# Unscaled operands for a seven-product gated MLP: the sums move into attention's last projection, and GpSimd stops computing there

## The chip, the core and the metric

The kernel runs on one core of a Trainium2 chip. It computes a small decoder trunk on 512 tokens. The metric is the device time of one execution in microseconds (us), given as the median of several runs.

A core has several engines that run side by side, each with its own list of instructions: TensorE (PE in the profile) multiplies matrices and has a separate step that loads weights (PEld); VectorE (DVE) and ScalarE (ACT) compute element by element; GpSimd (POOL) can compute too and issues some of the transfers; SyncE (SP) issues the others. Engines wait for each other by semaphores. On-chip memory has 128 partitions, so a tile "128x512" holds 128 rows of 512 numbers. Products are summed up in PSUM, a memory of its own from which DVE and ACT read.

## The reference

Two layers. The first has a mixer (a linear recurrence and a pooling branch), the second a convolution module in its place, and each layer goes on with cross-attention and a gated MLP. The change lies in the MLP and in the last projection of attention. Cut to these:

```python
def rms_norm(x, g):
    y = x * lax.rsqrt(jnp.mean(x * x, axis=-1, keepdims=True) + EPS)
    return y * g

def cross_attn(x, mem, norm, mem_norm, wq, wk, wv, wo):
    ...
    o = jnp.einsum('bhqk,bkhd->bqhd', p, v).reshape(Bn, S, D_MODEL)
    return o @ wo

def conv_ffn(x, norm, w_up, dw_w, dw_b, w_down):
    h = rms_norm(x, norm) @ w_up
    g = causal_dwconv(h[..., :D_FF], dw_w, dw_b)      # width 3
    u = h[..., D_FF:]
    return (jax.nn.gelu(g) * u) @ w_down

for layer in range(2):
    x = x + (mixer_ab if layer == 0 else conformer_conv)(x, ...)
    x = x + cross_attn(x, ...)
    x = x + conv_ffn(x, ...)
return rms_norm(x, final_norm)
```

The width of the model is 1024, that of the MLP 3072, the tokens are 512. All is float32.

## The kernel before

**Layout and exactness.** Activations lie transposed: the residual stream is eight tiles `X[0]` to `X[7]`, each of 128 channels by 512 tokens. A float32 operand is split into a *high part* (a copy rounded to the type that PE takes, made by ACT at L162) and a *low part* (what the rounding left, a subtraction on DVE, or on POOL where the code asks for it, L163). `mm3` (L168 to L170) makes one product of three matmuls: high by high, high by low, low by high. A 512-token matmul has 512 columns, one of a half has 256.

**The norm.** Attention's last projection (`back`) adds each finished chunk to `X[n]` and feeds it to the next norm, `Norm.feed`: L189 makes the high part of gain times X, L190 its low part (both kept in `act` tiles as `norm.x`), and L198 sums the squares on DVE. `norm.x` does not hold the scale, the reciprocal root of the mean square, which is the same for all channels of a token. The scale `norm.r` is made later (`rstd`: a split of the sum, two matmuls with a matrix of 1/1024 at L229 and L230, a root on ACT at L255, a reciprocal on DVE), and what was computed from `norm.x` is multiplied by it afterwards.

**The MLP** (`ffn`) has 24 chunks of 128 gate channels and as many value channels. Chunks 0 to 3 are made in the *opening*: eight plain products `start(0)` to `start(7)`, gate and value of each chunk in turn, of 24 matmuls of 512 columns. Their weights are the pieces of `wup`: a load, a high part, a low part (L577, L580), the first two before the opening. Between the products stand the width-3 convolution (`tap_steps`), the GELU, the product with `norm.r` (on POOL) and that with the value.

Chunks 4 to 23 are made by one *unit* each, which computes gate and value together as a product of two-by-two blocks with seven block products instead of eight (Winograd's form of Strassen's scheme; the value's sign is turned, so that the weights need sums only). The weight blocks are a11, a12 (gate) and a21, a22 (value), of 512 channels; from them come s3 = a11 + a21, s1 = a21 + a22, s2 = s3 + a22, s4 = s2 + a12. These sums are made by DMAs that add into memory, issued on POOL (L543 to L549), each as soon as the block before it has been split; the raw tile that holds a11 is overwritten by s3, s2 and s4 in turn, the one that holds a21 by s1. The operands on the other side are blocks of 512 channels by 256 tokens: B11, B21, B22, and the sums T1 = B11 - B12, T3 = B22 - B12, T2 = -T3 - B11 and T4 = -T2 - B21 (rows are halves of the channels, columns halves of the tokens). Class `Seven` makes all seven in the opening, from X times gain *times the scale* (`operand`, L478 to L508): eight scaled chunks (L493), two differences on POOL, two on DVE, and the high and low parts of all seven, those of T1 to T4 with their low parts on POOL. They lie in 14 of the 15 `big` tiles.

A unit's block products come in the order B11, B21, T2, T3, T1, B22, T4 (`m(...)`), 12 matmuls of 256 columns each; DVE combines their results by halves (L610). Between T3 and T1, and behind T4, stand two *down products* of 12 matmuls of 512 columns, which multiply finished chunks with a piece of `wdown` and add to X. So a unit has 84 matmuls of 256 columns and 24 of 512. Each slot between two products also splits blocks for the next units (`ahead`: high part on ACT, low part on DVE, sum DMA on POOL).

**What sets the order.** Inside `ffn` the order on PE, ACT, DVE and POOL is the order of the program text (`manual_schedule`); SP's loads, and everything outside, are ordered by a planner with priorities. Each of these engines works strictly in its order, so that one instruction that waits holds up all behind it on that engine. Tiles come from pools that are reused in turn: 32 `act` tiles, 15 `big` tiles, four `whi` and four `wlo`, three `raw`, eight `tmp`, five PSUM tiles `mm` and two `aux`.

**GpSimd** computes in the opening (low parts of weight blocks, products with the scale, differences, low parts of T1 to T4) and in the second layer's convolution module. In the units it only issues the sum DMAs.

Of the kernel before, what the change touches and what calls it, by code (L numbers as in the profile page):

```python
# [58 lines left out]
def trunk(ctx: ExitStack, tc: tile.TileContext, I: dict, out: list):  # L59
# [111 lines left out]

    def blk(w, i, n=P):
        hi, lo = w
# [51 lines left out]
    def mean_all(s, n=T):  # L225

        hi, lo = split(s, act_r()[:, :n], act_r()[:, :n])
# [146 lines left out]
    def attention(layer, norm, mem, nxt):  # L374
# [82 lines left out]
        back(0, range(4, 6))  # L457
        back(1, range(6))
        transpose(3)
        back(2, range(6))  # L460
        mix(3)
        for n in range(3):
            back(n, range(6, C))
        for n in range(3, C):
            back(n, range(C))


    class Seven:
# [6 lines left out]
        def __init__(self, norm):  # L475
            self.norm = norm
            self.x = [(big_r(), big_r()) for _ in range(7)]

        def operand(self, h):

            two = lambda t: t.rearrange("p (a b) -> p a b", a=2)
            f = [big_f(), wp.tile([P, D], F32, tag="wlo", name=nm("scaled"))]
            at = slice(h * T, (h + 1) * T)
            t1, t2, t3, t4 = [two(tmp_f()) for _ in range(4)]
            (b11, b12), (b21, b22) = [(two(t)[:, :, :M], two(t)[:, :, M:]) for t in f]

            def part(j, t, eng=None):
                split(t, two(self.x[j][0][:, at]), two(self.x[j][1][:, at]), eng)

            for k in range(2):  # L490
                for i in range(2):
                    c = 4 * k + 2 * h + i
                    V.scalar_tensor_tensor(  # L493
                        f[k][:, i * T : (i + 1) * T], X[c], col(self.norm.gain[0], self.norm.gain[1] + c), self.norm.r,
                        op0=ALU.mult, op1=ALU.mult,
                    )
            G.tensor_tensor(t3, b22, b12, op=ALU.subtract)
            G.tensor_tensor(t1, b11, b12, op=ALU.subtract)
            yield
            part(self.B11, b11)  # L500
            part(self.B21, b21)
            part(self.B22, b22)
            yield
            V.scalar_tensor_tensor(t2, t3, -1.0, b11, op0=ALU.mult, op1=ALU.subtract)
            V.scalar_tensor_tensor(t4, t2, -1.0, b21, op0=ALU.mult, op1=ALU.subtract)
            part(self.T2, t2, G)
            part(self.T3, t3, G)
            yield  # L508
            part(self.T1, t1, G)
            part(self.T4, t4, G)  # L510

        def product(self, ps, w, j):
            for c in range(4):
                at = slice(c * M, (c + 1) * M)
                mm3(ps, blk(w, c * P), (self.x[j][0][:, at], self.x[j][1][:, at]), c == 0, c == 3)
            return ps

    class Blocks:
# [15 lines left out]
        def part(self, name, eng=None):  # L534
# [4 lines left out]
            of = {"a12": self.a12, "a22": self.a22, "s1": self.z}.get(name, self.r)  # L539
            self.w[name] = split(of, self.hi[:, at], self.lo[:, at], eng) if at else split(of, eng=eng)  # L540
# [10 lines left out]
    def ffn(layer, norm, nxt):  # L551
        ys = {}

        def taps_of(c, g):
            y = tmp_f()
            for _ in tap_steps(c, g, y):
                pass
            return y

        def tap_steps(c, g, y):  # L560
            dw = lambda j: col("f_dw_w", (layer * 3 + j) * CF + c)
            A.activation(y, g, AF.Identity, scale=dw(2), bias=col("f_dw_b", layer * CF + c))
            yield
            for s in (1, 2):
                V.scalar_tensor_tensor(y[:, s:], g[:, : T - s], dw(2 - s), y[:, s:], op0=ALU.mult, op1=ALU.add)  # L565
            yield
# [775 lines left out]
```

## Time and profile before

| | |
|---|---|
| time, median of 3 runs | 1500.24 us (1499.22 to 1501.97) |
| the profiled execution | 1499.24 us |
| its span in the trace | 1497.5 us |
| mean granted clock of PE | 0.99 |
| PE busy | 1457.3 us (97%), 8388 matmuls |
| DVE busy | 1102.4 us (74%) |
| ACT busy | 729.3 us (49%) |
| POOL busy | 344.5 us (23%), 336 instructions |

Where the stages lie in the span of the trace: attention's last projection of the first layer ends at 365 us, the opening of the first MLP follows up to 418 us (the first matmul of the first unit starts at 418.02), then come its 20 units up to 738 us. The second layer's convolution module and attention follow, and its MLP begins at 1093.5 us.

How to read the rows. A row of a single instruction gives its start and its duration in us, the engine, the line of the kernel, the operation, the program's names (written from <- read) and the shapes; what it waited for stands in brackets at the end, with the waiting time. A row of a group gives the number of instructions and three numbers in ns: the shortest, the middle and the longest. A row "a <- b: x, n, y" of the waits says that instructions of kind a waited for b for x us in sum, n times, y at the longest. Busy times of an engine are shares of the span; only the time in which nothing else could go on is worth anything when it is removed.

### The profile page before, as it was taken

Reading aid. Unit: us, or ns where it says so; the run is one execution under the profiler, and the core shown is the slowest. Engines: PE = TensorE matmul, PEld = TensorE weight load, DVE = VectorE, ACT = ScalarE, POOL = GpSimd, SP = SyncE. Lnnn points to the kernel's source line nnn. Section 1 sums busy time; section 2 is a strip of 40 time slices with the busy share of each in tenths; the row PEclk is TensorE's granted clock in tenths of the full one; section 3 lists DMA queues with packets and bytes.
Section 4 is the critical chain, followed back from the end, with each engine's and each line's share of the span. In section 5 each row is a group of like instructions: output and inputs, shape, how many; then the busy total and the mean of one; then the engine's idle time right before and its main releaser. Section 6 shows DMA issues by size and latency. Waiting matters only on the chain.

```text
span 1497.5 us, 21974 instructions
## 1 busy us (share of the span) xinstructions
PE 1457.3 (97%) x8388; PEld 1260.8 (84%) x8388; DVE 1102.4 (74%) x1684; ACT 729.3 (49%) x1162; POOL 344.5 (23%) x336
## 2 busy tenths in 40 slices
PE   8999999999989999999999998999998999999997
PEld 7988788887779999999887666888876999999997
DVE  7876765657878777777776995766678877877765
ACT  7568743434445444544445336544444444454433
POOL 0012310001542222222006852300036222222111
PEclk9999999999999999999999999999999999999999
DMA  8523233203257777776426653321233777877741
GB/s 298 162 87 97 85 126 99 71 28 112 72 145 180 168 170 164 187 164 154 136 97 176 162 162 109 112 97 57 71 84 98 184 169 159 179 181 164 171 119 57
DMA packets 75641, 198.99 MB, mean 133 GB/s; under 512 B 8464, under 2 KB 9488, under 8 KB 75536
## 3 DMA queue, kind: packets, MB, share of 16 engines
q1 hardware_dynamic: 52208, 155.36, 33.3%
q0 software_dynamic: 23040, 41.95, 16.7%
q8 instruction: 66, 1.08, 0.3%
q14 instruction: 39, 0.32, 0.1%
q10 hardware_dynamic: 288, 0.27, 0.1%
HBM read 145.13 MB, written 2.10 MB: 98 GB/s over the span
## 4 chain that ended last, share of the span: by engine, by line
PE 74%; DVE 7%; issue 5%; DMA 3%; ACT 3%; POOL 2%; SPq 0%; ACTq 0%; POOLq 0%; DVEq 0%
PE mm L168 18%; PE mm L170 18%; PE mm L169 18%; PE aux L168 6%; PE aux L169 6%; PE aux L170 6%; PE aux L1110 1%; DVE tmp L565 1%; DVE wlo L163 1%; DVE wlo L580 1%; DVE act L163 1%; DMA raw<-wa 1%; POOL tmp L701 1%; DMA big<-in_wdown 1%; ACT whi L162 1%
## 5 line engine op out<-in xcount | busy, mean ns | idle before, releaser
L170 PE MATMUL mm<-act,wlo 128*128 128x512 f32 (+1 forms) x829 | 323.4, 390 | 8.8 <-DVE wlo L580 6.2
L168 PE MATMUL mm<-act,whi 128*128 128x512 f32 (+1 forms) x829 | 323.6, 392 | 0.5 <-ACT act L162 0.5
L169 PE MATMUL mm<-act,whi 128*128 128x512 f32 (+1 forms) x829 | 323.1, 390 | 0.0
L168 PE MATMUL mm<-bigr,act 128*128 128x256 f32 x832 | 237.1, 285 | 2.2 <-DVE tmp L610 1.9
L162 ACT ACTIVATE whi<-raw 128x1024 fp32r<-128x1024 f32 (+1 forms) x161 | 152.0, 948 | 178.7 <-PE mm L169 94.9
L169 PE MATMUL mm<-bigr,act 128*128 128x256 f32 x832 | 237.1, 285 | 0.0
L170 PE MATMUL mm<-bigr,act 128*128 128x256 f32 x832 | 236.7, 284 | 0.0
L170 PEld LDWEIGHTS mm<-act,wlo 128*128 128x128 f32 x829 | 156.8, 189 | 42.6 <-DVE wlo L580 7.9
L168 PEld LDWEIGHTS mm<-act,whi 128*128 128x128 f32 x829 | 156.7, 189 | 37.8 <-issue 3.3
L163 DVE TENSOR_TENSOR wlo<-raw,whi 128x1024 fp32r<-128x1024 f32 (+1 forms) x139 | 152.5, 1102 | 43.6 <-ACT whi L162 41.5
L169 PEld LDWEIGHTS mm<-act,whi 128*128 128x128 f32 x829 | 156.8, 189 | 32.1 <-DVE act L163 1.3
L162 ACT ACTIVATE act<-raw 128x512 fp32r<-128x512 f32 x176 | 108.5, 623 | 154.0 <-DMA raw<-raw 103.0
L168 PEld LDWEIGHTS mm<-bigr,act 128*128 128x128 f32 x832 | 160.9, 193 | 4.6 <-issue 2.2
L169 PEld LDWEIGHTS mm<-bigr,act 128*128 128x128 f32 x832 | 161.0, 193 | 1.9 <-issue 0.2
L168 PE MATMUL aux<-act,whi 128*128 128x512 f32 x407 | 159.8, 393 | 2.6 <-ACT act L162 1.3
L170 PE MATMUL aux<-act,wlo 128*128 128x512 f32 x407 | 158.8, 390 | 3.3 <-DVE wlo L163 3.3
L169 PE MATMUL aux<-act,whi 128*128 128x512 f32 x407 | 159.6, 392 | 2.3 <-DVE act L163 2.3
L170 PEld LDWEIGHTS mm<-bigr,act 128*128 128x128 f32 x832 | 160.9, 193 | 0.2 <-issue 0.2
L163 POOL TENSOR_TENSOR wlo<-raw,whi 128x1024 fp32r<-128x1024 f32 (+1 forms) x22 | 51.8, 2366 | 415.2 <-ACT whi L162 415.1
L163 DVE TENSOR_TENSOR act<-raw,act 128x512 fp32r<-128x512 f32 x162 | 111.2, 688 | 37.8 <-ACT act L162 37.2
L610 DVE TENSOR_TENSOR tmp<-mm,tmp 128x256 f32<-128x256 f32 x280 | 113.5, 419 | 2.1 <-PE mm L170 2.1
L169 PE MATMUL mm<-bigr,whi 128*128 128x256 f32 x392 | 111.0, 283 | 0.0
(269 smaller groups left out, 2714.3 us busy)
## 6 DMA issues: line engine op xcount, KB each, us to landing
raw<-wa POOLq DMA_DIRECT2D x120, 256.0 KB, 5.0
big<-in_wdown SPq DMA_DIRECT2D x42, 512.0 KB, 5.4
wa<-in_wpair SPq DMA_DIRECT2D x80, 256.0 KB, 4.2
raw<-in_wpair SPq DMA_DIRECT2D x40, 512.0 KB, 5.1
raw<-in_pw SPq DMA_DIRECT2D x24, 512.0 KB, 3.7
raw<-in_win SPq DMA_DIRECT2D x20, 512.0 KB, 3.3
raw<-raw POOLq DMA_DIRECT2D x40, 256.0 KB, 4.4
raw<-in_wv SPq DMA_DIRECT2D x16, 512.0 KB, 5.2
```

The source lines that it names most:

```text
L162: A.activation(hi, src, AF.Copy)
L163: (eng or V).tensor_tensor(lo, src, hi.bitcast(F32), op=ALU.subtract)
L168: PE.matmul(ps, wh, xh, start=first, stop=False)
L169: PE.matmul(ps, wh, xl, start=False, stop=False)
L170: PE.matmul(ps, wl, xh, start=False, stop=last)
L565: V.scalar_tensor_tensor(y[:, s:], g[:, : T - s], dw(2 - s), y[:, s:], op0=ALU.mult, op1=ALU.add)
L580: V.tensor_tensor(w[2], w[0], w[1].bitcast(F32), op=ALU.subtract)
L610: V.tensor_tensor(out, a, b, op=ALU.add)
L701: G.tensor_tensor(y[c], y[c], norm.r, op=ALU.mult)
L1110: return PE.matmul(accs[c][32 * j : 32 * j + 32, s:], taps[c][:, 4 * g + j], hs[c][1][j][:, : T - s], start=s == 0, stop=g == PE_GROUPS[c] ...
```

## The change

It has five parts.

1. *Operands without the scale.* B11, B21 and B22 are no longer made: `product` takes halves of `norm.x`, which exists anyway (chunks 0 to 3 and 4 to 7 are the two halves of the channels, columns 0 to 255 and 256 to 511 those of the tokens). T1 to T4 are made from gain times X without the scale. The scale is then applied in each unit to the combined gate and value, two products of 512 columns on DVE (L616 and L620 of the changed kernel).
2. *The sums in attention's last projection.* `sums(k)` makes one quarter (128 of 512 channels) of all four T operands from chunks k and k + 4. The projection ends its chunks in the order 0, 4, 1, 5, 2, 6, 3, 7, and behind each of the first three pairs stands one call; the fourth call is in the opening, behind `start(4)`. The split of the sum of squares is made ahead of `start(0)`.
3. *No arithmetic on GpSimd in the MLP.* Low parts, products with the scale and differences go to DVE; POOL issues DMAs only.
4. *High parts ahead of low parts.* `part` is split into `high` (ACT) and `low` (DVE and the sum DMA), and in most slots the text has the high parts first, or a slot earlier than the low parts. The weight pieces get a class `Piece` with the same two halves. The s blocks now lie in `big` tiles, both parts in one, where they were two `act` tiles.
5. *Pieces of work carried over.* The gating of a chunk is a generator, `left`, of which the next unit runs the rest; the sum of a down product with X is carried as `due`. The next raw load of a unit moves from behind product B11 to behind T3.

The core of the diff:

```diff
@@ back, behind the scores and mixes
+        seven = Seven(nxt)
+        for k in range(4):
+            for n in (k, k + 4):
+                back(n, range(6 if n in acc else 0, C))
+            if k < 3:
+                for _ in seven.sums(k):
+                    pass
+        return seven
@@ class Seven
-            self.x = [(big_r(), big_r()) for _ in range(7)]
+            self.t = [(big_r(), big_r()) for _ in range(4)]
-        def operand(self, h):
...
+        def sums(self, k):
+            f = [tmp_f(), tmp_f()]
+            for i in range(2):
+                c = k + 4 * i
+                A.activation(f[i], X[c], AF.Copy, scale=col(self.norm.gain[0], self.norm.gain[1] + c))
+            (b11, b12), (b21, b22) = [(x[:, :M], x[:, M:]) for x in f]
+            t13, t24 = tmp_f(), tmp_f()
+            t1, t3, t2, t4 = t13[:, :M], t13[:, M:], t24[:, :M], t24[:, M:]
+            V.tensor_tensor(t3, b22, b12, op=ALU.subtract)
+            V.tensor_tensor(t1, b11, b12, op=ALU.subtract)
             V.scalar_tensor_tensor(t2, t3, -1.0, b11, op0=ALU.mult, op1=ALU.subtract)
             V.scalar_tensor_tensor(t4, t2, -1.0, b21, op0=ALU.mult, op1=ALU.subtract)
+            at = slice(k * M, (k + 1) * M)
+            for (hi, _), t in zip(self.t, (t1, t2, t3, t4)):
+                A.activation(hi[:, at], t, AF.Copy)
             yield
+            for (hi, lo), t in zip(self.t, (t1, t2, t3, t4)):
+                V.tensor_tensor(lo[:, at], t, hi[:, at].bitcast(F32), op=ALU.subtract)
 
         def product(self, ps, w, j):
             for c in range(4):
-                at = slice(c * M, (c + 1) * M)
-                mm3(ps, blk(w, c * P), (self.x[j][0][:, at], self.x[j][1][:, at]), c == 0, c == 3)
+                if j >= self.T1:
+                    x = blk(self.t[j - self.T1], c * M, M)
+                else:
+                    x = blk(self.norm.x[c if j == self.B11 else c + 4], M if j == self.B22 else 0, M)
+                mm3(ps, blk(w, c * P), x, c == 0, c == 3)
@@ class Blocks: part(name, eng) becomes high(name) and low(name)
+                both = big_r()
+                self.w[name] = both[:, :T], both[:, T:]
+            A.activation(self.w[name][0], self.block(name), AF.Copy)
...
+        def low(self, name):
+            hi, lo = self.w[name]
+            V.tensor_tensor(lo, self.block(name), hi.bitcast(F32), op=ALU.subtract)
             if name == "a11":
                 G.dma_start(self.r, self.z, accum_op=ALU.add)
...
@@ ffn: the gating of a unit's chunk
+        def gating(c, f, g, ps, u3):
+            y = tmp_f()
+            V.tensor_tensor(g, g, norm.r, op=ALU.mult)
+            A.activation(y, g, AF.Identity, scale=dw(2), bias=col("f_dw_b", layer * CF + c))
+            yield
+            add(f[:, :M], ps, u3)
+            V.tensor_tensor(f, f, norm.r, op=ALU.mult)
...
@@ unit: the slots of the first products
             ps = m(seven.B11, "a11")
-            if c - 1 in last:
-                last.pop(c - 1)()
-            ahead(c, "s4")
-            if c + 3 in pairs:
-                pairs[c + 3].load()
-            if c + 2 in pairs:
-                pairs[c + 2].load_second()
+            next(left, None)
             A.activation(m1, ps, AF.Copy)
+            high(c + 1, "s3")
+            high(c + 1, "a22")
+            if due:
+                due()
+            next(left, None)
 
             ps = m(seven.B21, "a12")
+            low(c + 1, "s3")
+            low(c + 1, "a22")
...
             ps = m(seven.T2, "s2")
+            high(c, "s4")
+            high(c + 2, "a11")
+            high(c + 1, "a12")
             add(u2, ps, m1)
+            low(c, "s4")
...
@@ opening
+            ss = split(norm.ss)
             start(0)
             fetch(2)
-            low(w[-1])
-            for name in ("a11", "a12", "a22"):
-                ahead(first, name, G)
-            norm.r = rstd(norm.ss)
+            w[-1].low()
+            for name in ("a11", "a22", "a12"):
+                high(first, name)
+                low(first, name)
+            norm.r = scale_of(mean_of(ss))
...
             start(4)
             fetch(6)
+            w[-1].low()
             values(1)
-            low(w[-1])
+            t = seven.sums(3)
+            next(t)
             close(1)
-            next(steps, None)
-            steps = seven.operand(1)
-            next(steps)
+            next(t, None)
```

More of the change, by code (lines that the diff above doesn't have):

```diff
@@ L549, in part, with ffn @@
                 G.dma_start(self.r, self.a12, accum_op=ALU.add)
[L551 removed]
+    def ffn(layer, norm, nxt, seven):
         ys = {}
[L554 to L566, printed above, removed]
[L567 to L586 removed]
         class Down:
@@ L796, in ffn @@
                 unit(c)
-            last.pop(CF - 1)()
+            due()
+            for _ in left:
+                pass
         if nxt:
```

275 lines of the change are left out of this document (138 added, 137 removed).

## The prediction

> **What bounds the kernel now.** I read the page first, then the table of stretches, then who PE waited for, then single instructions around those waits.
>
> ```profile
> span 1497.5 us, 21974 instructions
> ...
> PE 1457.3 (97%) x8388; PEld 1260.8 (84%) x8388; DVE 1102.4 (74%) x1684; ACT 729.3 (49%) x1162; POOL 344.5 (23%) x336
> ```
>
> PE is busy nearly all the time, so only time that PE loses can be won. The stretches say where it loses (columns: stretch, its length, busy time and count of PE, of weight loads, DVE, ACT and POOL, granted clock, DMA share, GB/s):
>
> ```profile
> 343.00:365.00 22.00, 22.00 (x99) 18.23 (x98) 14.15 (x19) 9.98 (x15) 0.00 (x0) 1.00 0.38 123
> 364.00:452.00 88.00, 77.31 (x377) 64.38 (x376) 68.67 (x75) 39.99 (x63) 43.30 (x33) 0.94 0.40 102
> 452.00:514.00 62.00, 62.00 (x433) 58.07 (x432) 51.45 (x93) 31.64 (x54) 15.54 (x18) 1.00 0.77 179
> 514.00:576.00 62.00, 62.00 (x433) 58.07 (x432) 48.29 (x85) 28.44 (x48) 13.81 (x16) 1.00 0.76 164
> ```
>
> Attention's last projection (343 to 365) and the units (452 to 576, 108 matmuls each, so 15.5 us a unit) lose nothing. The opening of the first FFN (364 to 452) does. The second FFN does the same, so PE's waits over the whole span come in pairs (total, times, longest):
>
> ```profile
> PE mm L170 <- DVE wlo L580: 6.2, 2, 3.1
> ...
> PE aux L170 <- DVE wlo L163: 3.3, 2, 1.6
> PE stat L229 <- ACT act L162: 3.1, 2, 1.6
> ...
> PE aux L169 <- DVE act L163: 2.3, 2, 1.1
> PE mm L168 <- DVE tmp L610: 1.9, 2, 1.5
> ...
> PE mm L168 <- ACT act L162: 0.5, 1, 0.5
> ```
>
> How much an opening loses: its first matmul, and the first of product T2 in the second unit, before which the last wait lies, start here in the two FFNs; the other four rows give the pitch where nothing waits.
>
> ```profile
> 364.91 0.39 PE L168 MATMUL mm<-act,whi 128*128 128x512 f32 x1
> ...
> 445.21 0.35 PE L168 MATMUL mm<-bigr,act 128*128 128x256 f32 x1 [1.55 <-DVE tmp L610]
> ...
> 639.78 0.28 PE L168 MATMUL mm<-bigr,act 128*128 128x256 f32 x1
> ...
> 641.82 0.28 PE L170 MATMUL mm<-bigr,act 128*128 128x256 f32 x1
> ...
> 738.05 0.39 PE L168 MATMUL mm<-act,whi 128*128 128x512 f32 x1
> ...
> 740.77 0.39 PE L168 MATMUL mm<-act,whi 128*128 128x512 f32 x1
> ...
> 1093.53 0.39 PE L168 MATMUL mm<-act,whi 128*128 128x512 f32 x1
> ...
> 1171.17 0.36 PE L168 MATMUL mm<-bigr,act 128*128 128x256 f32 x1 [0.30 <-DVE tmp L610]
> ```
>
> Seventeen starts in 2.04 us and twelve in 2.72: pitches of 0.120 us at 256 columns and 0.227 at 512 (84 and 24 of them make the unit's 15.5). An opening up to that T2 holds 218 matmuls of 512 columns (192 of the plain products, 2 of the mean, 24 of the first unit) and 108 of 256: 62.4 us. It took 80.3 and 77.6. Lost are 17.9 and 15.2, together 33.1 us. More than half is waiting proper; a part is clock, which the throttle halves behind the waits:
>
> ```profile
> 374.20:377.40 3.20, 3.20 (x9) 2.53 (x8) 2.00 (x1) 2.11 (x3) 0.00 (x0) 0.50 0.14 24
> 411.80:414.60 2.80, 2.80 (x8) 2.19 (x7) 2.77 (x3) 0.62 (x2) 2.50 (x3) 0.50 0.56 187
> 432.20:435.20 3.00, 3.00 (x16) 3.00 (x15) 2.94 (x6) 0.50 (x1) 0.95 (x2) 0.50 0.77 162
> ```
>
> With two more in the second opening, at 1139 and 1159, that is some 15 us at clock 0.50, or 7.5 lost.
>
> Why DVE is late there: POOL computes beside it and stretches it.
>
> ```profile
> L198 DVE TENSOR_TENSOR tmp<-tmp,tmp x28: 677/687/3957, 204.8 to 1096.1; 128x512 f32<-128x512 f32 x28
> ...
> L493 DVE SCALAR_TENSOR_TENSOR big<-x,par,r x8: 739/1259/1782, 383.7 to 1132.9; 128x512 f32<-128x512 f32 x8
> ```
>
> ```profile
> 367.41 3.96 DVE L198 TENSOR_TENSOR tmp<-tmp,tmp 128x512 f32<-128x512 f32 x1
> ```
>
> ```profile
> 369.27 1.54 POOL L163 TENSOR_TENSOR act<-wa,act 128x512 fp32r<-128x512 f32 x1
> ```
>
> The norm's last sum takes 3.96 us instead of 0.69 while POOL makes three low parts, so the mean is late at 370. Later the scaled operands (8 of L493 in an opening) and POOL's own queue delay a piece's low part at 408, and the first unit's blocks after that.
>
> **The change, part by part.** *POOL's arithmetic.* An opening has 22 such instructions: 6 low parts of blocks, 4 products with the norm's scale, 4 differences, 8 low parts of T operands. The first ten go to DVE at its unstretched pitch, 0.60 us by the starts here (0.69 long, overlapping by 0.09):
>
> ```profile
> 443.11 0.69 DVE L163 TENSOR_TENSOR act<-raw,act 128x512 fp32r<-128x512 f32 x1
> 443.71 0.69 DVE L163 TENSOR_TENSOR wlo<-wa,whi 128x512 fp32r<-128x512 f32 x1
> ```
>
> That is +6.0 us of DVE in an opening. It loses there 8 scaled operands (0.65), 4 T sums and 6 low parts (0.60): -11.2. The opening gets lighter on DVE even before the stretching ends.
>
> *T sums in the projection.* Three of four groups move there, each with 8 half-width DVE instructions and on ACT 2 scaled copies and 4 half copies:
>
> ```profile
> L610 DVE TENSOR_TENSOR tmp<-mm,tmp 128x256 f32<-128x256 f32 x280 | 113.5, 419 | 2.1 <-PE mm L170 2.1
> ```
>
> ```profile
> 337.55 0.71 ACT L189 ACTIVATE act<-x,par 128x512 fp32r<-128x512 f32 x1
> ...
> 373.39 1.28 ACT L255 ACT_TABLE_LOAD   x1 [1.36 <-PE stat L230]
> ```
>
> DVE: 8 x (0.42 - 0.09) = 2.6 us; ACT: 2x0.71 + 4x0.36 (half) = 2.9. A group comes with two pieces of wo, 48 matmuls, 10.9 us. From 343 to 365 DVE is 64% and ACT 45% busy; this makes them 88% and 72%: covered by back's matmuls. Without that cover it would cost 6 groups x 2.6 = 16 us. The pieces' new order (0, 4, 1, 5, 2, 6, 3, 7) leaves PE the same matmuls, and X 7 still ends the stage: 0.
>
> *The mean.* From the row at 367.41: the sum ends at 368.1, its halves at 368.8 and 369.5, ahead of PE's 370.1; the wait for the mean goes. ACT then makes four high parts (until 371.4) before the root's table load and the root (373.3), DVE four low parts (372.7) before the reciprocal of 3.3 us: the scale is there at 376.6.
>
> *The plain products.* PE starts one every 5.45 us; is each piece's low part there? Adding up DVE's and ACT's order of the built program with these durations, those of the third to eighth piece end at 370.9, 377.7, 385.6, 387.4, 393.1 and 399.9, and are wanted at 376.3, 381.7, 387.2, 392.6, 398.1 and 403.5. The tightest is the fifth, with 1.6 us. Its path: s1's high part waits on ACT for two accumulating DMAs one after the other (a22's adds to z, which a11's must have read), the second queued on POOL behind the first; behind s1 stand the GELU with its table load, the product with the scale, the value product, and then the piece.
>
> ```profile
> L543 POOL DMA_DIRECT2D raw<-raw x40: 852/862/1010, 367.3 to 1423.3; - x40
> ...
> DMA to landing us min/median/max: 3.3/4.4/7.4
> ```
>
> ```profile
> L545 POOL DMA_DIRECT2D raw<-wa x40: 858/859/1210, 371.8 to 1426.9; - x40
> ...
> DMA to landing us min/median/max: 3.2/4.1/7.0
> ```
>
> ```profile
> L547 POOL DMA_DIRECT2D raw<-wa x40: 850/860/885, 383.6 to 1430.9; - x40
> ...
> DMA to landing us min/median/max: 3.2/5.8/9.1
> ```
>
> With medians: a11's low part 371.5, first landing 376.0, second 380.6 (with 0.5 for its start), s1 high 381.1, table 382.4, GELU 383.0, two DVE products 384.4, low part 385.6. I take medians, the DMA engines being little used there (share 0.14 above). With both maxima it is 5.9 later, and PE waits 4.3 us. After the eighth product DVE is some 2.5 us behind PE, but nothing of the first unit is wanted so early: s4's low part ends at 415.3 and is used at 418.7, y of the fourth chunk 412.6 against 416.5.
>
> *The units.* New on DVE are two products with the scale (L616, L620): 48.29/4 + 2x0.60 = 13.3 of 15.5 us. Blocks go from act to big tiles; beside 8 T tiles the 15 are full, so s4's copy on ACT now waits for the end of product T2. Behind it stand the copies of a11, a12 and wdown, none wanted within the unit. From T2's end s4's low part takes 1.2 us and is wanted after T3, a down product and T1, 5.6: 4.4 to spare. s2 has room for a landing of 14 us (maximum 9.1), y has 3.4 us. On SP the next raw load moves from product B11 to behind T3, past the two wa loads; it is wanted 15 us later. POOL's queue keeps four DMA issues a unit, 4x0.86 of 15.5. So the units lose nothing: 0. With a margin gone, each us over costs 40 us.
>
> *Behind the last unit* of the first FFN, y is queued on DVE behind the low part of a wdown piece whose load starts late; I get 743.0 for its end against PE's need at 743.3, where PE waited 0.5 us (last row of the waits). Bounds -0.5 and +4 (one more load in front); taken: 0.
>
> *Clock.* With the waits the five half-clock stretches go, 7.5 us of the 33.1.
>
> **The sum.** The profiled execution took 1499.24 us, 1.0 below the median 1500.24 of the runs. 1499.24 - 33.1 + 1.0 (left for the mean's two matmuls and their neighbours, 0.5 an opening) = 1467.1, and 1.0 for the median: 1468 us.
>
> **The rivals.** *The fifth piece is late in both openings*, its two DMAs landing slowly: 4.3 us of waiting and 1.5 of half clock each, 1468 + 11.6 = 1480. For it: the chain is new at that place, and landings spread by a factor of two; against it, the idle DMA engines.
>
> *Three clock stretches stay.* Those at 374, 432 and 1159 follow only waits of up to 1.6 us. Had they a cause of their own, they would stay: 1468 + 3x1.5 = 1472.5. Against it: each stands right behind such waits, and from 452 to 576 the clock is 1.00. The Trainium skill speaks for this rival: "TensorE: Matmul & The Clock Gate", section "Why this matters for your kernels", puts the return to half clock at idle gaps of over about 3 us, and here only 411 and 1139 follow one (3.1 us).
>
> *The units get slower*, by the DMAs that feed s1, s2 and s4, issued on POOL beside a busier DVE. Once landings exceed 14 us every unit is late; 1 us in each of 40 gives 1508, and from 0.8 us (33.1/40) the kernel is slower than before. Against it: no landing above is over 9.1, and an issue took 0.86 us in the middle and 1.21 at most with DVE at 78 to 83%.
>
> *Nothing much comes of it*: the waits only move, into attention's projection (16 us above) and the first unit: 1484 to 1500. Against it stand the margins above.
>
> **How the numbers follow.** Forecast, 1463 to 1471: 0.66. Clock stretches stay, to 1475: 0.07. Fifth piece late, 1476 to 1484: 0.14. Nothing much: 0.05. Units slower: 0.08. Below, a loss of 33.1 and the 0.5 behind the last unit are all that is seen, 1466.7; I allow 3.7 for what the trace doesn't show: 1463. Up to 1482 some 0.17 is left out. A measurement of this kernel tells about 0.2% (3 us) from no change; faster by more has 0.89 (the first three cases and part of the fourth), the same 0.03, slower 0.08.
>
> **What would show it.** In the changed kernel's profile: no PE wait for the mean, for a piece of wup or for y in either opening; clock 1.00 from the first plain product on; each DVE form of one duration, L213's maximum 0.69; units still 15.5 us. I am wrong if PE waits for a piece behind a GELU, if PE waits in a unit for a bigr block, or if back's products wait for whi or wlo.

## The result, and the profile after

The changed kernel takes 1467.32 us (median of 4 runs, 1466.86 to 1468.02) against 1499.98 us of the kernel before, run beside it (1499.22 to 1501.97). The ratio is 0.9781, with a 95% interval of 0.9764 to 0.9798: 32.7 us or 2.2% faster. The forecast was 1468, with a range of 1463 to 1482. The profiled execution took 1466.86 us.

The head of the page of the changed kernel, with each engine's busy time:

```profile
span 1465.1 us, 22101 instructions
...
PE 1442.8 (98%) x8388; PEld 1253.4 (86%) x8388; DVE 1136.2 (78%) x1812; ACT 742.1 (51%) x1182; POOL 276.9 (19%) x292
```

PE has the same 8388 matmuls, DVE 128 instructions more, and POOL 44 fewer, the 22 of each opening. PE's busy time fell by 14.5 us without a matmul less, about half of it since a matmul at half clock counts as busy for longer (the prediction put some 7.5 us on that).

The table of stretches (length; busy time and count of PE, weight loads, DVE, ACT, POOL; granted clock, DMA share, GB/s): the end of attention's last projection, the first opening up to product T2 of the second unit, four units, and the second opening:

```profile
343.00:364.50 21.50, 21.50 (x97) 17.80 (x96) 20.16 (x40) 14.21 (x27) 0.00 (x0) 1.00 0.29 98
364.50:427.00 62.50, 62.50 (x328) 53.93 (x327) 49.87 (x73) 33.06 (x51) 7.89 (x9) 1.00 0.50 135
427.00:489.00 62.00, 62.00 (x432) 58.08 (x431) 54.12 (x94) 29.70 (x50) 13.91 (x16) 1.00 0.77 173
...
1075.60:1138.00 62.40, 62.40 (x328) 53.83 (x327) 49.55 (x73) 32.84 (x50) 7.76 (x9) 1.00 0.52 137
```

PE is busy from end to end in both openings, at clock 1.00. Measured as the prediction did, from the first plain product to T2 of the second unit (start, duration, engine, line):

```profile
364.47 0.39 PE L168 MATMUL mm<-act,whi 128*128 128x512 f32 x1
...
426.90 0.28 PE L168 MATMUL mm<-bigr,bigr 128*128 128x256 f32 x1
...
1075.50 0.39 PE L168 MATMUL mm<-act,whi 128*128 128x512 f32 x1
...
1137.93 0.28 PE L168 MATMUL mm<-bigr,bigr 128*128 128x256 f32 x1
```

Both are 62.43 us, where the pitches alone give 62.4. The 17.9 and 15.2 us are won whole. DVE's busy time in an opening is 50 of 62.5 us, so it has room; the projection before it is the fullest place (DVE 94%, ACT 66%). What PE still waits for lies elsewhere (total, times, longest):

```profile
PE stat L258 <- ACT actf L1193: 6.1, 1, 6.1
PE mm L170 <- DVE wlo L163: 3.1, 3, 1.4
...
PE mm L168 <- ACT act L628: 0.3, 1, 0.3
```

The first is the layer norm of the convolution module, which took 4.8 us before. The last is y at the end of the first MLP.

### The profile page after: what moved, and what is told of

Read it like the earlier page. It is cut to its first block, busy times and chain, and to the rows that moved or that the text cites. A ratio compares the mean times of both kernels' runs of the same rounds, so it can differ in the third digit from the quotient of the medians.

```text
span 1465.1 us, 22101 instructions
## 1 busy us (share of the span) xinstructions
PE 1442.8 (98%) x8388; PEld 1253.4 (86%) x8388; DVE 1136.2 (78%) x1812; ACT 742.1 (51%) x1182; POOL 276.9 (19%) x292
## 3 DMA queue, kind: packets, MB, share of 16 engines
q1 hardware_dynamic: 52208, 155.36, 33.1%
## 4 chain that ended last, share of the span: by engine, by line
PE 86%; issue 3%; DVE 2%; DMA 1%; ACT 1%; POOL 1%; SPq 0%; POOLq 0%; ACTq 0%
PE mm L168 22%; PE mm L170 22%; PE mm L169 21%; PE aux L168 6%; PE aux L169 6%; PE aux L170 6%; PE aux L1157 1%; DMA raw<-in_wv 1%; PE aux L436 0%; POOL tmp L1012 0%; DMA actf<-h 0%; DMA raw<-in_wdown 0%; DVE big L988 0%; DVE wlo L163 0%; ACT whi L162 0%
## 5 line engine op out<-in xcount | busy, mean ns | idle before, releaser
L170 PE MATMUL mm<-act,wlo 128*128 128x512 f32 (+2 forms) x1149 | 411.6, 358 | 2.5 <-DVE wlo L163 2.5
L168 PE MATMUL mm<-act,whi 128*128 128x512 f32 (+2 forms) x1149 | 412.1, 360 | 0.3 <-ACT act L628 0.3
L169 PE MATMUL mm<-act,whi 128*128 128x512 f32 (+2 forms) x1149 | 411.7, 359 | 0.0
L168 PEld LDWEIGHTS mm<-act,whi 128*128 128x128 f32 x1149 | 216.8, 189 | 38.9 <-issue 3.3
L169 PEld LDWEIGHTS mm<-act,whi 128*128 128x128 f32 x1149 | 217.0, 189 | 33.1 <-DVE act L163 0.9
L162 ACT ACTIVATE whi<-raw 128x1024 fp32r<-128x1024 f32 x121 | 127.2, 1056 | 170.5 <-PE mm L169 90.9
L170 PE MATMUL mm<-bigr,bigr 128*128 128x256 f32 x640 | 181.1, 283 | 0.0
L169 PE MATMUL mm<-bigr,bigr 128*128 128x256 f32 x640 | 181.1, 283 | 0.0
L168 PE MATMUL mm<-bigr,bigr 128*128 128x256 f32 x640 | 180.9, 283 | 0.0
L556 ACT ACTIVATE bigr<-raw 128x512 fp32r<-128x512 f32 x160 | 100.5, 629 | 154.2 <-DMA raw<-wa 55.9
L163 DVE TENSOR_TENSOR wlo<-raw,whi 128x1024 fp32r<-128x1024 f32 x101 | 126.3, 1255 | 40.7 <-ACT whi L162 38.5
L563 DVE TENSOR_TENSOR bigr<-raw,bigr 128x512 fp32r<-128x512 f32 x160 | 109.9, 688 | 32.5 <-ACT bigr L556 30.3
L169 PEld LDWEIGHTS mm<-bigr,bigr 128*128 128x128 f32 x640 | 122.7, 192 | 1.6
L168 PEld LDWEIGHTS mm<-bigr,bigr 128*128 128x128 f32 x640 | 122.7, 192 | 1.6
L170 PEld LDWEIGHTS mm<-bigr,bigr 128*128 128x128 f32 x640 | 122.7, 192 | 0.0
L170 PEld LDWEIGHTS aux<-act,wlo 128*128 128x128 f32 x407 | 76.4, 188 | 16.5
```

The lines of the kernel that those rows point to most:

```text
L162: A.activation(hi, src, AF.Copy)
L163: (eng or V).tensor_tensor(lo, src, hi.bitcast(F32), op=ALU.subtract)
L168: PE.matmul(ps, wh, xh, start=first, stop=False)
L169: PE.matmul(ps, wh, xl, start=False, stop=False)
L170: PE.matmul(ps, wl, xh, start=False, stop=last)
L556: A.activation(self.w[name][0], self.block(name), AF.Copy)
```

## The experiments

All times are medians; each kernel was run beside the kernel before, which took 1499.5 to 1500.5 in these sets. The traces differ by up to 1.2 us in their first 40 us, where all these kernels do the same, so differences under that are not read.

The theory was that GpSimd's arithmetic made DVE late in the openings. The rivals: that the gain comes from what DVE no longer does there, or from the order of high and low parts.

**GpSimd's arithmetic given to DVE, and nothing else** (kernel before, label before_dve).

```diff
-            G.tensor_tensor(t3, b22, b12, op=ALU.subtract)
+            V.tensor_tensor(t3, b22, b12, op=ALU.subtract)
...
-            part(self.T2, t2, G)
+            part(self.T2, t2)
...
             for name in ("a11", "a12", "a22"):
-                ahead(first, name, G)
+                ahead(first, name)
```

> The kernel before, with nothing changed but the engine of the 22 arithmetic instructions that GpSimd does in each opening: DVE does them, in their places in the text. Theory A (the openings lost their 33 us to GpSimd: it stretched DVE's instructions beside it, and its own results came late): DVE's forms go back to one duration each, the mean's wait goes, and although DVE gets 13.2 us more work in an opening (22 x 0.60, some 59 us in all of the 62.4 that PE needs), more than half of the loss is won: 1470 to 1483 us. Rival B (the gain comes from taking work off DVE in the opening: no scaled operands, sums made elsewhere): DVE is now the bound of the opening, and the time is 1490 us or more.

Measured: 1494.89 us, ratio 0.9969 (0.9957 to 0.9981). Only 5 of the 32.7 us are won, and rival B's bound is met. Stretches and waits of PE:

```profile
364.00:446.00 82.00, 70.08 (x359) 57.84 (x358) 63.53 (x93) 37.80 (x59) 9.61 (x11) 1.00 0.42 107
```

```profile
PE mm L170 <- DVE wlo L580: 8.8, 6, 2.4
...
PE mm L168 <- DVE tmp L610: 4.7, 3, 2.0
PE aux L170 <- DVE wlo L163: 3.3, 2, 1.6
```

The wait for the mean is gone, and so is the stretching in the openings, yet there are six waits for a piece's low part now, 8.8 us, where there were two of 6.2. DVE's busy time over the span hardly changed: 1096.8 us for 1728 instructions, against 1102.4 for 1684. So the 44 instructions that came over took about what the stretching had cost. Quiet GpSimd alone isn't the reason of the gain: with its work on DVE, DVE is late again.

Nor does the whole loss hang on it. The prediction measured an opening up to product T2 of the second unit. Its first part, the eight plain products, ends with the first unit's first matmul. In this kernel that matmul and that T2 start here:

```profile
415.37 0.28 PE L168 MATMUL mm<-bigr,whi 128*128 128x256 f32 x1
...
442.56 0.36 PE L168 MATMUL mm<-bigr,act 128*128 128x256 f32 x1 [1.99 <-DVE tmp L610]
```

The first unit's part takes 27.2 us, as in the kernel before (from 418.02 to 445.21), and 25.9 in the second opening, again in both kernels. The changed kernel needs 18.4 (from 408.47 to 426.90). So 16.3 of the 33.1 us are lost in that part, and taking the arithmetic off GpSimd changed nothing of them; the 5.6 us by which the openings of the two traces differ were all won in the plain products. Some of that loss is DVE's lag from the plain products: it ends the fourth chunk's y at 428.7, 13 us after the unit has begun. The two last waits, 2.9 us, come from something else. DVE stands still there, behind a copy on ACT that waits for a transfer:

```profile
437.12 0.63 ACT L162 ACTIVATE act<-raw 128x512 fp32r<-128x512 f32 x1 [6.26 <-DMA raw<-wa]
...
437.79 0.69 DVE L163 TENSOR_TENSOR act<-raw,act 128x512 fp32r<-128x512 f32 x1 [5.40 <-ACT act L162]
```

This is the next unit's s2, whose transfer is issued only when s3 has been split. In its first unit the kernel before splits s3 and s2 two slots apart; the changed kernel makes s3's high part a slot earlier, and s2's high and low part one and two slots later. So the order of the text is a rival for a part of this half of the gain, and no run changed that order alone.

**GpSimd kept busy with work that nobody reads** (changed kernel, label dummy).

```diff
+        def idle_work(t, n):
+            t = t.bitcast(F32)
+            for _ in range(n):
+                G.tensor_tensor(spare, t[:, :M], t[:, M : 2 * M], op=ALU.subtract)
...
+            idle_work(w[-1].hi, 8)        # behind the low part of each of five pieces
+            idle_work(norm.x[C - 1][0], 4)    # ahead of the split of the sum of squares
```

> The changed kernel, with 44 subtractions of 256 columns on GpSimd added to each opening, whose result nobody reads (4 behind the last chunk's high part, 8 behind the high part of each of five pieces of wup, which they read). This separates the two halves of theory A. If GpSimd's arithmetic hurts by stretching DVE's instructions beside it: DVE's forms in the opening get longer again (a piece's low part 1.4 us and more instead of 1.22, a sum over 1 us instead of 0.69), some 5 us of DVE in each opening, and PE waits where the slack is under that, at the fifth piece: 1469 to 1478 us. If it hurt only because its results came late: no form gets longer, 1466 to 1468.

Measured: 1490.55 us, 23.2 more than the changed kernel. Single instructions on DVE in the first opening (start, duration):

```profile
368.06 1.22 DVE L213 TENSOR_TENSOR tmp<-tmp,tmp 128x512 f32<-128x512 f32 x1
...
388.10 1.43 DVE L185 TENSOR_TENSOR wlo<-raw,whi 128x1024 fp32r<-128x1024 f32 x1
...
392.28 0.68 DVE L722 TENSOR_TENSOR tmp<-mm,r 128x512 f32<-128x512 f32 x1
...
407.98 3.53 DVE L519 TENSOR_TENSOR bigr<-tmp,bigr 128x256 fp32r<-128x256 f32 x4
```

The same four in the changed kernel, where GpSimd is quiet:

```profile
366.81 0.69 DVE L213 TENSOR_TENSOR tmp<-tmp,tmp 128x512 f32<-128x512 f32 x1
...
383.73 1.22 DVE L185 TENSOR_TENSOR wlo<-raw,whi 128x1024 fp32r<-128x1024 f32 x1
...
386.60 0.68 DVE L722 TENSOR_TENSOR tmp<-mm,r 128x512 f32<-128x512 f32 x1
...
397.24 1.43 DVE L519 TENSOR_TENSOR bigr<-tmp,bigr 128x256 fp32r<-128x256 f32 x4
```

The instructions with two inputs in on-chip memory get longer, by 1.2 to 2.5 times; the one whose first input is in PSUM (L722) does not. The Trainium skill, "SBUF — State Buffer", section "Who interferes with whom", has this rule: a DVE instruction with two SBUF inputs contends with a GpSimd instruction that reads SBUF. These rows agree with it, and show it without any dependence of DVE on GpSimd's result. So the half of the theory that concerned the stretching is shown. Its price here was above the expected range, since the four low parts of the sums at 408 (3.53 instead of 1.43) stand ahead of the eighth piece, for whose high and low part PE then waited up to 2.6 and 4.1 us, with half clock behind it. GpSimd's queue is part of it: s2's transfer was issued at 405.0, in place of 390.6. Nor are 23.2 us the price of the old arithmetic: the added work keeps GpSimd busy for 43.5 us in the first opening, where the 22 instructions of the kernel before took 34.5.

**Part of GpSimd's arithmetic put back** (changed kernel, label after_pool): the low parts of the first unit's blocks and the products of the GELU's result with the scale.

```diff
-                V.tensor_tensor(y[c], y[c], norm.r, op=ALU.mult)
+                G.tensor_tensor(y[c], y[c], norm.r, op=ALU.mult)
...
-                pairs[c].low(name)
+                pairs[c].low(name, G if norm.r is None or early else None)
```

> The changed kernel, with 9 or 10 instructions of each opening back on GpSimd: the low parts of the first unit's six blocks up to s2, and the four products of the GELU's result with the scale. All else as changed. Theory A (GpSimd's arithmetic as such costs the opening its time): about half of GpSimd's work is back, so about half of the loss is, 1478 to 1486 us, with waits of PE for a piece's low part. A weaker form of A (it costs only where a chain has no slack): the sum of squares is now ahead of these low parts and the fifth piece has 2.3 us, so 1468 to 1474. Rival B (it was DVE's load): 1466 to 1468, since DVE now has less to do than in the changed kernel.

Measured: 1472.49 us, 5.2 more. That is the weaker form: ten instructions on GpSimd, in place of DVE, cost 2.6 us an opening, at the fifth piece (0.9 us of waiting) and at y in the first unit.

**DVE's work put back: the scaled operands' share** (changed kernel, label load).

```diff
+        def more(n):
+            for _ in range(n):
+                V.tensor_tensor(norm.ss, norm.ss, norm.ss, op=ALU.max)
...
+            more(4)     # behind gate(0); 3 behind close(0), 4 behind sums(3), 3 in gate(2)
```

> The changed kernel, with 14 instructions more on DVE in each opening (512 columns, the maximum of the dead sum of squares with itself), as many as the scaled operands took there: 4 behind the first chunk's gating, 3 behind its low part, 4 behind the sums, 3 in the third chunk's gating. GpSimd stays quiet. After the first runs the theory is: DVE's work in the opening and GpSimd's stretching are two causes, each enough alone to make DVE late. In the run with the sums in the opening, 7.8 us of work more made PE lose 7.4 us. These 14 are 8.4 to 9.7 us: 5 to 9 lost in an opening, 1478 to 1486 us. Rival (what cost there was the sums' chain between ACT and DVE, not the work): 1467 to 1472.

Measured: 1479.31 us, 12.0 more, in the expected range. **The sums put back** (changed kernel, label sums_opening).

```diff
-            if k < 3:
-                for _ in seven.sums(k):
-                    pass
...
             close(0)
+            for k in range(2):
+                for _ in seven.sums(k):
+                    pass
...
             fetch(7)
             w[-1].low()
+            for _ in seven.sums(2):
+                pass
```

> The changed kernel, with the three groups of sums of the T operands that stand in attention's last projection moved into the opening: two behind start(2)'s gating, one behind the sixth piece's low part. Prediction's reading (the projection's matmuls cover them, the opening would not): each group takes DVE 2.6 us and, with its steps on ACT in between, 3.4 to 5; the piece for start(5) is then some 2 us late and the first unit's blocks come later too: 2 to 5 us an opening, 1471 to 1477 us. Rival (with GpSimd quiet DVE has room for them anywhere, since it is busy 50 of 63 us there): 1466 to 1469.

Measured: 1482.31 us, 15.0 more, above the 4 to 10 expected: behind the first late pieces come the waits of the first unit, for a piece of wdown and for y. **Both put back** (label load_sums, the two edits together).

> The same 14 instructions, and the three groups of sums in the opening too: the DVE work of the kernel before with all its GpSimd arithmetic on DVE, but in the changed kernel's order (high parts ahead, the sum of squares ahead, less carried in one slot). If the work is what counts, the time is that of that earlier run, 1493 to 1500 us. If the order of the text has a share of the gain in the openings, it is 1480 to 1490.

Measured: 1498.74 us, ratio 0.9990 (0.9981 to 0.9999). PE's waits there, the first of them for the high part of a piece, which ACT makes behind the work of the sums:

```profile
PE mm L168 <- ACT whi L182: 7.6, 2, 3.8
...
PE mm L170 <- DVE wlo L185: 5.3, 4, 2.4
```

That is nearly the kernel before, with GpSimd quiet and in the changed kernel's order of text. So the work taken off DVE is needed for nearly all of the gain: putting it back costs 12.0 and 15.0 us for its two halves, 31.4 for both. It does not follow that the order of the text earns nothing, for the loss lies elsewhere. The first unit's part takes 23.6 us here, against 27.2 in before_dve, and the plain products 54.5 against 50.3, with the sums now standing ahead of a piece's high part on ACT. The share of the order stays open.

**The sums behind the projection, without cover** (changed kernel, label sums_end).

```diff
+            for k in range(3):
+                for _ in seven.sums(k):
+                    pass
             ss = split(norm.ss)
             start(0)
```

> The changed kernel, with the same three groups of sums behind the projection in one go, in front of the split of the sum of squares, where no matmul covers them. The prediction gave 2.6 us for each of the six groups without cover, 16 us: 1483. With the steps on ACT in between a group is 3 to 4 us, the mean is late by some 10 and PE's clock is halved for some us behind it: 1485 to 1491. Rival (the sums' place doesn't matter): 1466 to 1470.

Measured: 1488.21 us, 20.9 more, as expected. In this kernel PE waits for the mean:

```profile
PE stat L247 <- ACT act L162: 14.8, 2, 7.4
```

The six groups cost 3.5 us each without cover, of which 2.5 are waiting; the rest is mostly clock (0.88 on the mean from 364 to 405).

**A longer chain ahead of the fifth piece** (changed kernel, label chain).

```diff
             elif name == "a22":
-                G.dma_start(self.z, self.a22, accum_op=ALU.add)
+                a22 = self.a22
+                if bounce:     # the first unit's a22 only
+                    a22 = act_f()
+                    G.dma_start(a22, self.z)
+                    G.dma_start(a22, self.a22)
+                G.dma_start(self.z, a22, accum_op=ALU.add)
```

> The changed kernel, with the second accumulating transfer ahead of s1 in each opening led through one more transfer (a22 is copied once before it is added), so that s1 is there some 4 to 5 us later. By the prediction's working this is the tightest path: GELU, two products and the fifth piece's low part follow on s1, with 2.3 us to spare as measured. PE then waits 2 to 3 us for that low part in each opening. Does the half clock follow such a single wait (the prediction took 1.5 us for it)? With it 1473 to 1477 us; without it 1471 to 1474. Rival (the chain isn't what the fifth piece hangs on): 1466 to 1468.

Measured: 1470.10 us, 2.8 more, somewhat under what was expected; in its trace 1.2 us of the difference lie in the first 40 us. s1's high part came 3.3 us later, not 4 to 5. The fifth piece's low part, and PE's first use of it, in that kernel:

```profile
387.59 1.22 DVE L185 TENSOR_TENSOR wlo<-raw,whi 128x1024 fp32r<-128x1024 f32 x1
```

```profile
388.86 0.50 PE L170 MATMUL mm<-act,wlo 128*128 128x512 f32 x1 [0.35 <-DVE wlo L185]
```

Take off the 1.2 by which this trace is late: the low part ends at 387.6 in place of 384.95, 2.7 later, and PE wanted it at 387.16. The chain is the tightest one, and its slack was 2.2 us. No half clock followed, but PE waited only 0.35 us, so that the question of the expectation (half clock behind a wait of 2 to 3 us) was not put.

**High parts right ahead of low parts** (changed kernel, label high_with_low): `low(name)` makes both; `high(name)` does nothing.

> The changed kernel, with the high part of each weight block made right ahead of its low part instead of a slot or some instructions earlier (blocks only; the pieces of wup and wdown stay as they are). Mine: DVE waits some 0.6 us for ACT at five places of a unit, 3 us against the 2.0 us that it idles in a unit now, of which part falls together with waits that it has anyway: 1467 to 1480 us, that is at most 0.3 us a unit. Rival C (high parts ahead of low parts carry a good part of the gain): 1490 us or more.

Measured: 1483.00 us, 15.7 more, between the two forecasts. The openings lose nothing; the units do:

```profile
PE aux L169 <- DVE act L634: 11.2, 8, 1.4
```

Eight waits for y, one in every fourth unit, where a new group of wdown begins and its first down product needs the chunk just made. **The same without the units' products with the scale** (label high_with_low_bare), two lines fewer in `gating`.

> The changed kernel with the blocks' high parts right ahead of their low parts, as in the earlier run, and without the two products with the scale in every unit (the scale is left out of the computation there). This tells why the high parts have to go ahead: the kernel before had them right ahead of the low parts and lost nothing in its units, but it had no scale products there. If these products are what makes the order necessary (1.2 us of DVE in a unit), the units lose nothing again: 1466 to 1469 us. If the other differences (blocks in big tiles, what is carried over) make it necessary, the loss of the earlier run stays: 1478 to 1483.

Measured: 1467.60 us, as expected if it is the products: the loss is gone. In the units the changed order is the price of the unscaled operands: their two products with the scale fill the units so that the high parts must go ahead.

**More work on DVE in every unit** (changed kernel, labels unit_plus2 and unit_plus4).

```diff
             V.tensor_tensor(f, f, norm.r, op=ALU.mult)
+            for _ in range(4):          # 2 in the other
+                V.tensor_tensor(f, f, f, op=ALU.max)
```

> The changed kernel, with four instructions more on DVE in every unit (512 columns, the maximum of the gated value with itself, which leaves it as it is), 0.60 to 0.69 us each. DVE idles 2.0 us of a unit's 15.5. The prediction has DVE's room at 2.2 and says that each us over costs 40 us: 2.4 to 2.8 us of work is 0.4 to 0.8 over, 1483 to 1499 us. Rival (part of DVE's idle time is waiting for PE's results and can't be used): more, 1500 to 1540. Rival (the room is larger, as idle time is counted with the overlap of instructions): 1467 to 1470.

> The changed kernel, with two instructions more on DVE in every unit instead of four: 1.2 to 1.4 us against the 2.0 that DVE idles. The prediction's room of 2.2 us holds it, and y's 3.4 us too: 1467 to 1470 us. If the room is smaller than the idle time because part of it is waiting for PE and ACT, each unit loses some 0.2 us and more: 1474 to 1484.

Measured: 1506.80 us with four, 39.5 more, or 0.99 a unit: not the 1483 to 1499 of the prediction's room, but the first rival, that a part of DVE's idle time can't be used. With two it is 1471.89 (1469.19 to 1473.10), 4.6 more and between the two forecasts. With four, DVE itself is the bound of the units:

```profile
452.00:514.00 62.00, 60.00 (x413) 55.40 (x412) 59.95 (x103) 24.88 (x43) 12.13 (x14) 1.00 0.69 160
```

With two it isn't, and PE still waits at some group beginnings. DVE's own idle time says why. The low part of s1 in the kernel with two more, and below it in the changed kernel, in the same unit:

```profile
470.96 0.69 DVE L563 TENSOR_TENSOR bigr<-raw,bigr 128x512 fp32r<-128x512 f32 x1 [2.03 <-ACT bigr L556]
```

```profile
467.79 0.69 DVE L563 TENSOR_TENSOR bigr<-raw,bigr 128x512 fp32r<-128x512 f32 x1
```

DVE gets late with a22's low part, behind it the transfer that makes s1, behind that s1's high part on ACT, and then DVE waits 2.03 us for work that it was itself late to start. The 2 us that DVE idles in a unit aren't room of 2 us.

**The clock.** No run was made for it, but the runs above hold single gaps of different length. PE's gap and the stretch behind it, in the kernel before_dve:

```profile
387.60:390.40 2.80, 0.38 (x3) 0.02 (x1) 2.80 (x5) 1.17 (x3) 0.00 (x0) 1.00 0.00 0
390.40:393.60 3.20, 3.20 (x14) 2.64 (x15) 3.20 (x6) 2.20 (x4) 0.00 (x0) 1.00 0.48 164
```

in the two openings of the kernel load:

```profile
404.90:408.10 3.20, 0.14 (x1) 0.00 (x0) 3.13 (x5) 0.00 (x0) 0.00 (x0) 1.00 0.00 0
408.10:411.20 3.10, 3.09 (x10) 2.46 (x11) 2.18 (x4) 0.84 (x2) 0.00 (x0) 0.72 0.50 164
...
1121.30:1124.50 3.20, 0.23 (x2) 0.00 (x0) 3.13 (x5) 0.00 (x0) 0.00 (x0) 1.00 0.00 0
1124.60:1128.00 3.40, 3.39 (x15) 2.82 (x16) 2.48 (x4) 1.15 (x2) 0.00 (x0) 1.00 0.47 159
```

and in the kernel dummy, where two gaps follow each other, of which the second has half clock from its start:

```profile
405.60:408.40 2.80, 0.16 (x2) 0.02 (x1) 2.80 (x3) 1.88 (x4) 2.64 (x4) 1.00 0.55 94
...
409.10:413.20 4.10, 0.39 (x1) 0.00 (x0) 4.10 (x5) 0.00 (x0) 3.79 (x5) 0.50 0.22 64
413.20:418.40 5.20, 5.16 (x12) 4.15 (x13) 3.53 (x4) 1.44 (x2) 4.81 (x6) 0.50 0.30 101
```

Counted from one start to the next, no half clock followed the gap of 2.8 us, and it followed that of 3.0 in dummy. Behind the two gaps of 3.5 in load it came once, in the first opening, and stayed away in the second. Gaps shorter than 2.8 give no clear answer either: in the kernel before there is a stretch of half clock at 374, behind gaps of 2.0 and 0.7 us, and none behind gaps of 1.9 and 0.7 at the same place in its second opening. So the length of the last gap does not decide alone; what else does is open. The Trainium skill, "TensorE: Matmul & The Clock Gate", section "Why this matters for your kernels", has the rule quoted in the prediction, of gaps over about 3 us; most of the longer gaps here agree with it, the second one in load does not.

## Why the prediction was right

*The time and the sum.* Right: 1467.3 against 1468, by the terms of the sum. The openings gave 33.1 us as predicted, and of the 1.0 us kept back nothing was needed. The spans differ by 32.4: ahead of the first opening 0.4 us were won too, between the openings 0.3 were lost (the convolution module's wait grew by 1.3, the rest got 1.0 shorter, and why is open), and behind the second 0.8.

*The plain products.* Right within 0.7 us. The ends of the low parts of the third to eighth piece were forecast at 370.9, 377.7, 385.6, 387.4, 393.1 and 399.9; they came at 370.4, 377.2, 384.95, 386.7, 392.6 and 399.8. The fifth was the tightest, as said, with 2.2 us where 1.6 were forecast: both accumulating transfers landed somewhat faster than the medians. The rival that it comes late did not happen. The chain's run shows that a delay costs PE what is over the slack; the 1.5 us of half clock that the prediction put on top of a wait of 4.3 us was not tested there.

*T sums in the projection.* Right: PE lost nothing from 343 to 364.5. DVE came to 94% there (88 forecast), ACT to 66% (72). "Without that cover 16 us" was too little as a price: it measured 20.9, since the 16 leave out the alternation with ACT and the clock. The price in the opening had not been put at all, and it is 15.0.

*The units.* Right that they lose nothing and that DVE needs 13.3 of 15.5 us (13.5 measured). The margins were overrated: y had 3.2 us (it ended at 475.5 and was used at 478.75), near the 3.4 forecast, but two instructions more, 1.4 us, already cost time in some units, since a delay of DVE comes back to it through the sum transfers. The room of 2.2 us was overrated too: four more instructions, 2.4 to 2.8 us, should have cost 0.2 to 0.6 us a unit by it and cost 0.99, so that some 1.4 to 1.8 us could be used (an estimate, the work less its cost).

*The clock.* Right: all five stretches went with the waits. The rival that three stay did not happen. Those at 411 and 1139 are 3.4 us long in the trace, so "some 15 us" for the five is a little low; the sum doesn't hang on it.

*Behind the eighth product and the last unit.* Near enough: s4's low part ended at 416.1 (415.3 forecast) and the fourth chunk's y at 413.4 (412.6), and neither held PE up; at the end of the first MLP PE waited 0.3 us for y where it had waited 0.5.

*The cause.* This step was right only in part, and the number doesn't speak for it: the sum takes the whole loss of the openings as won, whatever causes it. The prediction said "why DVE is late there: POOL computes beside it and stretches it", and treated the lighter opening on DVE as something that comes with it ("-11.2"). The stretching is real (the dummy run), but without it, with all the work on DVE, 28 to 31 of the 33 us stay lost (before_dve, load_sums). So DVE's own work, put back, is enough to lose nearly all of it, though not at the same places (load_sums). How much GpSimd's old arithmetic would cost beside the lighter DVE is known only in part: 5.2 us for ten of the 22 instructions, 23.2 for a heavier load that nobody reads. The gain needs both, a lighter DVE and a quiet GpSimd, and their prices don't add up. The first unit, whose blocks the prediction had delayed by the scaled operands and GpSimd's queue, was as slow without GpSimd's arithmetic; how much of that is work and how much the order of the text is open. The account of DVE's work (+6.0 and -11.2) also leaves out the fourth group of sums, 2.6 us by the prediction's own price, which stays in the opening: by it DVE gets lighter by 2.6 us there, not by 5.2.

*What would show it.* L213's maximum is 0.69 in both attentions, as said, but not over the whole span: one instance takes 2.88 us at 940.0 in the convolution module, where GpSimd goes on making low parts.

```profile
940.00 2.88 DVE L213 TENSOR_TENSOR tmp<-tmp,tmp 128x512 f32<-128x512 f32 x1
```

```profile
934.29 10.85 POOL L163 TENSOR_TENSOR wlo<-raw,whi 128x1024 fp32r<-128x1024 f32 x4 [12.31 <-ACT whi L162]
```

## What to carry to other kernels

A stretched instruction in the profile names a cause, not the only one: add up, without the stretching, what the engine has to do between two fixed points of the bounding engine, and try the removal alone before crediting it. Split the loss by stages too: here half of it lay in a stage that the removal did not touch. Room on an engine that feeds itself through transfers is less than its idle time; measure it by adding harmless instructions. Work moved under another stage's matmuls is worth the delay that it would cause where it stood, here, put back into the changed kernel, 0.95 us of PE for each us of DVE's sums (7.4 us an opening for 7.8), though DVE was busy only four fifths of the time.

## What was not expected of the hardware

Four half-width low parts took 3.53 us instead of 1.43 beside GpSimd's subtractions, a factor of 2.5, where a piece's low part took 1.2 to 1.9 times as long. So the short instructions suffered most in that run; why is open. And PE's half clock is no matter of the last gap alone: it followed one gap of 3.0 us, one of two gaps of 3.5, none of 2.8, and it sometimes came behind two shorter ones.
